# A two-block kernel: the second block's last input projections tied to the delta rule's scan by shared PSUM buffers, and the scan's right-hand side made by one VectorE operation

## The chip, the cores and the metric

The kernel runs on one core of a Trainium2 chip. The metric is the device time of one execution in microseconds, as the median of several runs; the kernel before is at 2178.66 us (three runs, 2176.99 to 2195.75).

## What is computed

Two transformer-like blocks run one after the other on 512 tokens of width 1024. Only the second block's mixer matters here. It projects the normalised tokens into the inputs of three branches (Hyena, gated linear attention or GLA, gated delta rule or GDN), runs the branches and concatenates their outputs. The delta rule works in chunks of 64 tokens, forward and backward at once, with four heads of 96 channels:

```python
rhs = concatenate([kb * exp(gcum), vc * bc])
sol = triangular_solve(eye - a, rhs, lower=True, unit_diagonal=True)
w, u = sol[..., :dk], sol[..., dk:]
v_new = u - w @ s
o = (qc * exp(gcum)) @ s + attn @ v_new
s_new = exp(g_last) * s + einsum('bhjd,bhje->bhde', kc * exp(g_last - gcum), v_new)
```

The state `s` goes from chunk to chunk, so the eight chunks of the 512 tokens follow one another. The kernel applies the inverse to `v - exp(gcum) * (k @ s)`, which is the right-hand side that the change is about.

## The kernel before, in words

The kernel is written as Python generators that emit instructions. `weave` (L331) takes steps from several generators in proportion to given weights, and so sets the order in which work is emitted. The framework then sets each engine's order within the limits of data and buffers: an instruction may be taken ahead of others that were emitted before it if its operands and its buffer are free. On the chip each engine, and the SyncE queue that issues the DMAs, runs its list strictly in order.

The second block's mixer is `mixer_in` (L2097). `side_proj` (L1899) makes 28 input projections of 128 output columns: nine for the delta rule, seven for GLA, then twelve more (`dg0` to `gg2`, six gates, and `hy0` to `hy5`, the Hyena inputs). One projection is `proj2`, which calls `gemm_cm` (L297): the weights of a block come by DMA into `wraw`, ScalarE rounds them (`wh`, L287), VectorE or GpSimd takes the rest (`wl`, L288), and 24 matmuls of 512 columns (lines 293 to 295, eight of each) sum into one PSUM tile `gps`. ScalarE and VectorE then make an activation or a short convolution (`cpad`, L1270; L1277, L1279) of it and a DMA writes it to DRAM.

PSUM tiles are taken by tag; each tag has two buffers, which rotate in the order of emission. `view` renames tags: the mixer's projections run on the view `w`, where "p" and "s" mean "g" and "i" means "p", while the delta rule runs on `v`, where each tag is itself. So before the change the projections sit in the tag "g" and the delta rule uses "p", "s" and "i": the two share nothing.

The first 16 projections and the preparation of keys, values and queries come first, then `gla_general` (behind branches that are not taken here), then `chain()`. It runs `gdn_solve` (L1416) for head pair 0 and then pair 1, and after that `gdn_scan` (L1455). A solve makes its matrices (`dps_`, `kkp`, `qkp`, all tag "p"), and `inverse` (L637) sends them through DRAM, runs 15 short steps of two VectorE operations each (L661, L662), sends the result back through DRAM and finishes with matmuls `ips` (L682). The scan does per chunk and head: `gxp` (keys times state, L1467), `gX` (two VectorE operations, L1470 and L1471), `gup` (inverse times `gX`, L1477), `vd_` and `vn_`, `gsp` (L1491), the new state `gSn` (L1494), and the output `gop` (L1502, L1504; tag "p"), which ScalarE and VectorE combine into `Og` and a DMA writes to `ogd` (L1507). `chain()` is woven with the remaining projections by the weights 192 and 66, after one projection that `next(side)` emits alone.

Behind the scan three generators are woven: GLA (`ttp`, `totp`, `sfp`, `cnp`, ...), `head_norm_out` of the delta rule's output (it loads `hO` from `ogd`, matmuls `ops` at L1949 and L1950), and the Hyena (tables `hraw`, L1818; inputs `hv` from `hud`, L1848; transposes `hyt`; transforms `dfp`; inverse transforms `hip`).

## Time and profile before

| what | us |
|---|---|
| median of three runs | 2178.66 |
| the profiled execution, its own time | 2177.16 |
| its span in the profile | 2175.4 |
| TensorE busy in the span | 1954.9 |
| VectorE busy in the span | 1136.3 |
| last result of the second inverse (`TQ`) starts, from the span's start | 1505.6 |
| last matmul of the scan starts, from the span's start | 1598.5 |
| first load of the stage after the mixer's weave (`g1r`) issues | 1719.0 |

The times on the timeline are from the span's start. The span lies 1.8 us inside the execution's own time, which is 1.5 us under the median. TensorE's busy time tells little by itself, since its clock has two levels, and small matmuls count as busy at either.

### The profile page before, as it was taken

How to read it: one execution, taken by the hardware profiler on the slowest of the kernel's cores; microseconds unless marked ns; L12 is line 12 of the kernel's file. 1: busy time of each engine (PE TensorE's matmuls, PEld its weight loads, DVE VectorE, ACT ScalarE, POOL GpSimd, SP SyncE). 2: the span in 40 equal slices, each digit the busy share in tenths (PEclk: the TensorE clock that was granted, in tenths of full speed). 3: DMA queues.
4: the chain of work that ended last, by engine and by line, in shares of the span. 5: the costliest groups of instructions: out<-in, count | busy, mean ns of one | idle time of the engine just before them, and what ended most of it. 6: DMA issues, size and time to landing. Idle time of an engine off the chain costs nothing. (4 is left out here: it accounts for less than half of the span.)

```text
span 2175.4 us, 37783 instructions
## 1 busy us (share of the span) xinstructions
PE 1954.9 (90%) x15280; PEld 1427.1 (66%) x15280; DVE 1136.3 (52%) x2542; ACT 719.2 (33%) x1390; POOL 245.5 (11%) x254
## 2 busy tenths in 40 slices
PE   7899999999698889988999487899999789999997
PEld 6676767666466764444524266677667577898897
DVE  4565645563362545455461487487456675434433
ACT  4333223333262433121322365422153234312321
POOL 0101011110100211111000031130002150010000
PEclk9999989999799989999999798999579899999999
DMA  6424232432854549979687433332152342333332
GB/s 160 145 61 131 82 102 65 126 111 75 183 175 158 165 133 322 327 262 328 244 300 251 181 116 103 104 81 80 44 171 62 127 144 76 97 93 93 97 92 74
DMA packets 177123, 312.21 MB, mean 144 GB/s; under 512 B 78648, under 2 KB 95816, under 8 KB 176938
## 3 DMA queue, kind: packets, MB, share of 16 engines
q1 hardware_dynamic: 167274, 291.84, 42.6%
q0 software_dynamic: 6784, 10.51, 1.7%
q10 hardware_dynamic: 2880, 7.34, 1.1%
q8 instruction: 123, 2.02, 0.4%
q14 instruction: 62, 0.51, 0.1%
HBM read 278.23 MB, written 39.77 MB: 146 GB/s over the span
## 5 line engine op out<-in xcount | busy, mean ns | idle before, releaser
L288 DVE TENSOR_TENSOR wl<-wraw,wh 128x1024 fp32r<-128x1024 f32 (+2 forms) x215 | 227.9, 1062 | 235.7 <-ACT wh L287 235.3
L287 ACT ACTIVATE wh<-wraw 128x512 fp32r<-128x512 f32 (+2 forms) x233 | 195.7, 844 | 251.7 <-PE gpt L326 136.9
L293 PE MATMUL gps<-hh,wh 128*128 128x512 f32 x568 | 235.2, 415 | 0.4 <-DVE kS L380 0.4
L294 PE MATMUL gps<-hh,wl 128*128 128x512 f32 x568 | 232.5, 410 | 1.2 <-DVE wl L288 1.2
L295 PE MATMUL gps<-hl,wh 128*128 128x512 f32 x568 | 233.0, 411 | 0.0
L1178 PE MATMUL hps<-w,xT 128*64 128x512 f32 x512 | 142.4, 611 | 3.3 <-DMA w<-in_w_moe 3.2
L324 PE MATMUL gpt<-wh,mh 128*128 128x256 f32 x512 | 142.9, 279 | 0.0
L325 PE MATMUL gpt<-wl,mh 128*128 128x256 f32 x512 | 142.9, 279 | 0.0
L326 PE MATMUL gpt<-wh,ml 128*128 128x256 f32 x512 | 142.9, 279 | 0.0
L293 PEld LDWEIGHTS gps<-hh,wh 128*128 128x128 f32 x568 | 108.2, 191 | 29.5 <-issue 2.9
L294 PEld LDWEIGHTS gps<-hh,wl 128*128 128x128 f32 x568 | 107.9, 190 | 29.5 <-DVE wl L288 4.2
L295 PEld LDWEIGHTS gps<-hl,wh 128*128 128x128 f32 x568 | 107.7, 190 | 25.7 <-issue 2.0
L293 PE MATMUL gps<-lhh,wh 128*128 128x512 f32 x232 | 98.0, 424 | 16.7 <-ACT wh L287 6.2
L294 PE MATMUL gps<-lhh,wl 128*128 128x512 f32 x232 | 96.2, 416 | 3.8 <-DVE wl L288 2.2
L324 PEld LDWEIGHTS gpt<-wh,mh 128*128 128x128 f32 x512 | 96.2, 188 | 0.1
L325 PEld LDWEIGHTS gpt<-wl,mh 128*128 128x128 f32 x512 | 96.2, 188 | 0.1
L326 PEld LDWEIGHTS gpt<-wh,ml 128*128 128x128 f32 x512 | 96.2, 188 | 0.0
L295 PE MATMUL gps<-lhl,wh 128*128 128x512 f32 x232 | 95.4, 413 | 0.0
L2003 POOL TENSOR_TENSOR x<-x,xev 128x512 f32<-128x512 f32 x36 | 50.2, 1403 | 388.3 <-DVE xev L2001 388.0
L1178 PEld LDWEIGHTS hps<-w,xT 128*64 128x64 f32 x512 | 36.9, 138 | 66.2 <-issue 50.8
L1279 DVE SCALAR_TENSOR_TENSOR cout<-cpad,cw,cout 128x512 f32<-128x512 f32 (+1 forms) x90 | 66.9, 743 | 2.1
L2019 DVE TENSOR_TENSOR uld<-uld 128x512 f32<-128x512 f32 x32 | 22.2, 693 | 87.3 <-ACT uld L2018 87.3
(1181 smaller groups left out, 4226.9 us busy)
## 6 DMA issues: line engine op xcount, KB each, us to landing
w<-in_w_moe SPq DMA_DIRECT2D x192, 512.0 KB
wraw<-in_w_modb SPq DMA_DIRECT2D x48, 512.0 KB
wraw<-in_w_in_2b SPq DMA_DIRECT2D x41, 512.0 KB
wraw<-in_w_mlp1b SPq DMA_DIRECT2D x32, 512.0 KB
wraw<-in_w_mlp2b SPq DMA_DIRECT2D x32, 512.0 KB
wraw<-in_w_inb SPq DMA_DIRECT2D x31, 512.0 KB
bm<-in_c_bias SPq DMA_DIRECT2D x16, 256.0 KB
wraw<-in_w_inb ACTq DMA_DIRECT2D x8, 512.0 KB
```

The source lines that it names most:

```text
L287: nc.scalar.activation(wh, raw[:, o:o + g], AF.Copy)
L288: self.we.tensor_sub(wl, raw[:, o:o + g], wh)
L293: nc.tensor.matmul(ps, wh, hh, start=first, stop=False)
L294: nc.tensor.matmul(ps, wl, hh, start=False, stop=False)
L295: nc.tensor.matmul(ps, wh, hl, start=False, stop=last)
L324: nc.tensor.matmul(ps, hh[:, g, sl], wh[:, k], start=f, stop=False, skip_group_check=True)
L325: nc.tensor.matmul(ps, hh[:, g, sl], wl[:, k], start=False, stop=False, skip_group_check=True)
L326: nc.tensor.matmul(ps, hl[:, g, sl], wh[:, k], start=False, stop=l, skip_group_check=True)
L1178: nc.tensor.matmul(ps[q], xT[:, 4 * kh + k, q], self.parts[h][:, 512 * (k - 2 * c):512 * (k - 2 * c) + 512], start=kh == 0 and k == 0, sto ...
L1279: nc.vector.scalar_tensor_tensor(ov[:n], pv[:n, :, j:j + L], wcol[:n, j:j + 1], ov[:n], op0=OP.mult, op1=OP.add)
L2003: (nc.gpsimd if last is None or cb < 3 else nc.vector).tensor_add(o, o, t)
L2019: nc.vector.tensor_mul(f, f, f)
```

## The change

Three edits. In `gdn_scan` the negated decays `nG` are made once per call on GpSimd, and the scan's right-hand side is made by one VectorE operation, `gX = xp * nG + v`, where there were two. In `side_proj` the projections from the seventeenth on (those emitted when 16 are there) take the tag "i", which on the view `w` is the tag "p" of the delta rule: their PSUM tiles rotate with `dps_`, `kkp`, `qkp` and `gop`. In `mixer_in` the single `next(side)` ahead of the weave is gone and the weights are 192 to 72.

```diff
--- before.py
+++ after.py
@@ -1459,6 +1459,8 @@
         n = len(heads)
         qs = [slice(64 * d, 64 * d + 64) for d in range(2)]
         St = [self.gS[:, hd[0]] for hd in heads]
+        nG = pool.tile([128, S, 4], F32, name="gnG")
+        nc.gpsimd.tensor_scalar(nG, eG, -1.0, None, op0=OP.mult)
         for c in range(S):
             X, vd, vn = [], [], []
             for i, (h, kT, qT, k, v, E, TQ) in enumerate(heads):
@@ -1467,8 +1469,7 @@
                     nc.tensor.matmul(xp[q], kT[:, c, q], St[i][:, d], start=True, stop=True)
                 x = pool.tile([128, 96], F32, name="gX", bufs=4)
 
-                nc.vector.tensor_scalar(x, xp, eG[:, c, h:h + 1], None, op0=OP.mult)
-                nc.vector.tensor_sub(x, v[:, c], x)
+                nc.vector.scalar_tensor_tensor(x, xp, nG[:, c, h:h + 1], v[:, c], op0=OP.mult, op1=OP.add)
                 X.append(x)
             yield n
             for i, (h, kT, qT, k, v, E, TQ) in enumerate(heads):
@@ -1906,7 +1907,7 @@
             self.we = nc.gpsimd if n in GDN_BLOCKS else nc.vector
             if n == "gk0":
                 pool = later()
-            ps = self.proj2(n, 128, T)
+            ps = self.gemm_cm("w_in_2b", W2.get(n, n), self.hh, self.hl, T, tag="i" if len(self.there) >= 16 else "g")
             if n in GDN_BLOCKS:
                 i = GDN_BLOCKS.index(n)
                 y, d = self.conv_silu(pool, ps, 128, 8, 64, self.cw[:, (i + 6) % 9]), self.cvd[i]
@@ -2149,8 +2150,7 @@
                                 heads.extend((2 * hp + e, kT[:, e], st["q"][:, 2 * hp + e], kv[:, :, e], kv[:, :, 2 + e], E[:, e], TQ[e])
                                              for e in range(2))
                         yield from v.gdn_scan(8, gs, heads, st["g"], self.ogd)
-                    next(side)
-                    self.run(self.weave((chain(), 192), (side, 66)))
+                    self.run(self.weave((chain(), 192), (side, 72)))
                     self.far.close()
                     self.oa = self.ox.enter_context(tp(name="oa", bufs=1, side="right")).tile([128, 8, 384], F32, name="oa")
                     nc.sync.dma_start(self.oa, self.oad.rearrange("c p d -> p c d"))
```

How the order moves. The first place is TensorE ahead of the matmuls `ips` that end the second inverse (pair 1); `gps` are the projections. Before:

```order
L295 MATMUL gps<-lhl,wh 128x512
L293 MATMUL gps<-lhh,wh 128x512
L294 MATMUL gps<-lhh,wl 128x512
L295 MATMUL gps<-lhl,wh 128x512
L682 MATMUL ips<-qv,No 64x64 x32
L682 MATMUL ips<-qv,Z 64x64 x32
L682 MATMUL ips<-W,Z 64x64 x64
L1477 MATMUL gup<-gX,TQ_14195 64x96 x2
L1491 MATMUL gsp<-vd__14284,kv_12336 96x96
```

and of the change, from the end of the first inverse on:

```order
L1478 MATMUL gup<-gX,TQ_13805 64x96 x2
L1478 MATMUL gup<-gX,TQ_13824 64x96 x2
L1503 MATMUL gop<-gS,qT__12141 64x96 x4
L1505 MATMUL gop<-vn__14233,E_13409 64x96 x2
L1505 MATMUL gop<-vn__14240,E_13409 64x96 x2
L1503 MATMUL gop<-gS,qT__12141 64x96 x4
L682 MATMUL ips<-qv,No 64x64 x32
L682 MATMUL ips<-qv,Z 64x64 x32
L682 MATMUL ips<-W,Z 64x64 x64
L1478 MATMUL gup<-gX,TQ_14183 64x96 x2
L1492 MATMUL gsp<-vd__14231,kv_12324 96x96
```

Before, a run of projection matmuls (106 from the last `gop` on, of which four are shown) stands ahead of the second `ips`; now none stands between the `gop` of the first chunk and these `ips`.

The second place is TensorE within one of the later chunks (`gup`, `gsp`, `gop`, `gxp` belong to the scan). Before:

```order
L1477 MATMUL gup<-gX,TQ_13817 64x96 x2
L1477 MATMUL gup<-gX,TQ_13836 64x96 x2
L1491 MATMUL gsp<-vd__14856,kv_12336 96x96 x2
L1477 MATMUL gup<-gX,TQ_14195 64x96 x2
L1504 MATMUL gop<-vn__14858,E_13460 64x96 x2
L1491 MATMUL gsp<-vd__14863,kv_12336 96x96
L1477 MATMUL gup<-gX,TQ_14214 64x96 x2
L1491 MATMUL gsp<-vd__14863,kv_12336 96x96
```

and of the change:

```order
L293 MATMUL gps<-lhh,wh 128x512
L294 MATMUL gps<-lhh,wl 128x512
L295 MATMUL gps<-lhl,wh 128x512
L1478 MATMUL gup<-gX,TQ_13824 64x96 x2
L293 MATMUL gps<-lhh,wh 128x512
L1492 MATMUL gsp<-vd__14976,kv_12324 96x96
L1478 MATMUL gup<-gX,TQ_14183 64x96 x2
L1492 MATMUL gsp<-vd__14976,kv_12324 96x96
L294 MATMUL gps<-lhh,wl 128x512
L1478 MATMUL gup<-gX,TQ_14202 64x96 x2
L1492 MATMUL gsp<-vd__14983,kv_12324 96x96
L295 MATMUL gps<-lhl,wh 128x512
```

Before, the scan's matmuls of chunks 4 to 7 follow one another alone; now 24 projection matmuls lie in each of the chunks 0 to 6, singly among the scan's and in a run at the end of the chunk. In all 288 projection matmuls now stand behind the branches of `gla_general`, where 255 stood.

The third place is SyncE's queue at the end of the scan (`ogd<-Og` is the delta rule's output; `hO` its load; `hv` the Hyena's input). Before:

```order
L1848 DMA hv_15548<-hud 128x512
L1848 DMA hv_15549<-hud 128x512
L2105 DMA lsc<-gv0d 128x512
L1507 DMA ogd<-Og 128x384
L2105 DMA lsc<-gv1d 128x512
L1818 DMA hraw<-in_c_dft 128x512 x2
L2105 DMA lsc<-gv2d 128x512
L1936 DMA hsg_15446<-sgd 128x512
L1936 DMA hsg_15448<-sgd 128x512
L1936 DMA hsg_15450<-sgd 128x512
L1942 DMA hO<-ogd 128x384 x8
L1818 DMA hraw<-in_c_dft 128x512 x2
```

and of the change:

```order
L1508 DMA ogd<-Og 128x384
L2106 DMA lsc<-gv1d 128x512
L1819 DMA hraw<-in_c_dft 128x512
L1586 DMA ls<-lsd 128x1024
L2106 DMA lsc<-gv2d 128x512
L1937 DMA hsg_15404<-sgd 128x512
L1937 DMA hsg_15406<-sgd 128x512
L1937 DMA hsg_15408<-sgd 128x512
L1943 DMA hO<-ogd 128x384 x8
L1819 DMA hraw<-in_c_dft 128x512 x2
L1846 DMA hdk<-in_hy_d 128x2x1 x2
L1849 DMA hv_15506<-hud 128x512
```

Before, the loads of `hv` were issued ahead of the scan's last output, and on TensorE the Hyena's `hyt` and 27 of its `dfp` matmuls stood ahead of the first `ops`. Now `hv` stands behind the eight loads of `hO`, and on TensorE `hyt` and all `dfp` stand behind all 16 `ops`.

## Rows read from the trace of the kernel before

**Rows 1.** the page: the span, and the clock granted to TensorE in 40 slices (tenths)

```profile
span 2175.4 us, 37783 instructions
...
PEclk9999989999799989999999798999579899999999
```

**Rows 2.** windows, scan without projections: PE, weight loads, DVE, ACT, POOL, clock, DMA

```profile
1560.00:1580.00 20.00, 20.00 (x137) 13.22 (x137) 9.55 (x39) 4.13 (x14) 0.00 (x0) 0.50 0.03 11
```

**Rows 3.** windows of 2 us where the clock falls, same columns

```profile
1520.00:1522.00 2.00, 2.00 (x15) 1.40 (x14) 0.80 (x4) 0.23 (x1) 0.00 (x0) 1.00 0.04 8
...
1524.00:1526.00 2.00, 2.00 (x8) 1.19 (x9) 0.36 (x2) 0.00 (x0) 0.00 (x0) 0.50 0.27 98
```

**Rows 4.** the chain that ended last, one chunk to the next, no projections between

```profile
1557.34 1.00 PE gup L1477 x8
...
1568.97 1.00 PE gup L1477 x8
```

**Rows 5.** TensorE timeline: two projection matmuls in a row, then chunks at full clock

```profile
1494.12 0.39 PE L293 MATMUL gps<-lhh,wh 128*128 128x512 f32 x1
1494.35 0.39 PE L294 MATMUL gps<-lhh,wl 128*128 128x512 f32 x1
...
1505.39 0.38 PE L1477 MATMUL gup<-gX,TQ 64*64 64x96 f32 x4
...
1516.64 0.38 PE L1477 MATMUL gup<-gX,TQ 64*64 64x96 f32 x4
...
1517.12 0.50 PE L293 MATMUL gps<-lhh,wh 128*128 128x512 f32 x1
```

**Rows 6.** windows of line 293 alone (every third projection matmul)

```profile
1408.00:1599.40 191.40, 36.10 (x85) 16.38 (x85) 0.79 0.24 68
...
1505.40:1516.60 11.20, 2.01 (x4) 0.74 (x4) 1.00 0.05 18
```

**Rows 7.** VectorE groups during the second inverse (1471.6 to 1487.7): count, busy, mean

```profile
L661 DVE SCALAR_TENSOR_TENSOR tmp<-q,n 128x1 f32<-128x1 f32 (+14 forms) x15 | 4.6, 303 | 2.7 <-DMA n<-nd 2.4
...
L1279 DVE SCALAR_TENSOR_TENSOR sg<-cpad,hcw,sg 128x512 f32<-128x512 f32 x6 | 4.5, 748 | 0.0
...
L662 DVE TENSOR_REDUCE q<-tmp 128x1 f32<-128x1 f32 (+14 forms) x15 | 3.6, 238 | 0.3
...
L288 DVE TENSOR_TENSOR wl<-wraw,wh 128x512 fp32r<-128x512 f32 x5 | 3.4, 687 | 0.0
```

**Rows 8.** VectorE timeline: second inverse starts, its last copy, its last result

```profile
1471.61 0.16 DVE L661 SCALAR_TENSOR_TENSOR tmp<-q,n 128x1 f32<-128x1 f32 x1 [2.40 <-DMA n<-nd]
...
1487.30 0.37 DVE L663 COPY q<-q 128x256 f32<-128x256 f32 x1
...
1505.58 0.69 DVE L702 TENSOR_TENSOR TQ<-ips,qv 128x512 f32<-128x512 f32 x1 [0.24 <-PE ips L682]
```

**Rows 9.** tile view of gX and gsp: ns min/median/max

```profile
L1470 DVE TENSOR_SCALAR gX<-gxp,eG x48: 301/311/320, 908.1 to 1592.9; 128x96 f32<-128x96 f32 x48
...
L1471 DVE TENSOR_TENSOR gX<-kv,gX x48: 241/251/259, 908.4 to 1593.3; 128x96 f32<-128x96 f32 x48
...
L1494 DVE SCALAR_TENSOR_TENSOR gSn<-gSn,eC,gsp x64: 298/309/311, 916.5 to 1588.7; 96x96 f32<-96x96 f32 x64
```

**Rows 10.** timelines of SyncE queue and TensorE behind the scan

```profile
1604.67 6.19 SPq L1942 DMA_DIRECT2D hO<-ogd  x8
...
1599.57 1.08 PE L1858 MATMUL hyt<-ct,hv 128*128 128x128 f32 x4 [0.61 <-DMA hv<-hud]
...
1604.98 0.56 PE L293 MATMUL dfp<-yth,dh 128*128 128x256 f32 x1
...
1611.05 0.86 PE L1949 MATMUL ops<-hO,ct 128*64 128x384 f32 x2 [0.28 <-DMA hO<-ogd]
```

**Rows 11.** windows: the stage behind, once its transforms run

```profile
1622.40:1719.20 96.80, 91.01 (x843) 70.21 (x843) 70.51 (x176) 30.89 (x63) 19.73 (x18) 0.98 0.21 64
```

**Rows 12.** windows: TensorE starting after a pause

```profile
1410.00:1414.00 4.00, 3.65 (x15) 1.86 (x17) 1.04 (x3) 0.89 (x2) 0.00 (x0) 0.53 0.03 8
```

## The prediction

> **What bounds the kernel now.** I read the page first, for where the clock is low. The change touches the second block's mixer, 1410 to 1600 us of a span of 2175.4 us, and the slice of the page that begins at 1523 us has the lowest digit of its PEclk line [rows 1]. The windows say why it matters: with no projections left, TensorE works without a gap at a granted clock of 0.50, the lower of its two levels (1.2 GHz) [rows 2]. It falls after 1522 us [rows 3], about 5 us after the last projections that lie between the chunks' small matmuls (1517.12) [rows 5].
>
> The chain that ended last then shows the scan. One chunk follows the other at a period of 1568.97 - 1557.34 = 11.63 us at the low level [rows 4]. At the full level (2.4 GHz) and with 12 projection matmuls inside, one took 1516.64 - 1505.39 = 11.25 us [rows 5]. Two such matmuls in a row are 0.23 us apart there [rows 5], so the 12 cost 2.8 and the rest of the chunk about 8.5. The scan thus has a small price per chunk at the full clock and pays nearly 12 because little else is left to keep the clock. Line 293 is every third projection matmul: 85 ran between 1408 and 1599.4, 255 projections in all, but only four (12) in that first chunk [rows 6].
>
> Ahead of the scan stands the second inverse. Its 15 steps lie on VectorE, from 1471.61 to 1487.30, and its last `TQ` starts at 1505.58 and ends 0.7 us later [rows 8]. The VectorE groups of that stretch show the steps' own two operations with 4.6 and 3.6 us, and the projections' convolutions and weight splits between them with 4.5 and 3.4 [rows 7].
>
> So three stretches decide: until the second `TQ`, from there to the scan's end at 1599.0 (last matmul at 1598.5 and its half microsecond), and the stage behind, which ends at 1719.0.
>
> **Part 1, until the second `TQ`.** Projections leave the second inverse. VectorE's steps alone are 4.6 + 3.6 = 8.2 us of 15.7 [rows 7, 8], so up to 7.5 us go. Against that, 24 instead of 12 projections stand ahead of one of the first solve's small matmuls: 12 x 0.23 = +2.8 us. TensorE is also idle for some 20 us of the second inverse, and starts its `ips` at the low level: after an earlier pause a window of 4 us had a clock of 0.53 [rows 12]. The `ips` are 8 us of matmuls at the full level, of which the first part would double; I take +2 (0 to +8). The 33 projections that are now behind the branches instead of ahead (33 x 0.23 = 7.6 us) I value at -1: the low clock just behind the branches [rows 12] says that TensorE had paused ahead of them, so it was not what they waited for; -7.6 is the other end. Sum: -7.5 + 2.8 + 2 - 1 = -3.7. The chain from the inverse through DRAM has fewer other transfers beside it, for which I allow 2 more: **-6** (-12 to 0).
>
> **Part 2, the scan.** After the change 24 projections lie in each of the first seven chunks. At the full clock a period is 8.5 + 24 x 0.23 (5.5) = 14.0 us. The merged right-hand side takes one operation out of each of 48 pairs. The two cost 311 and 251 ns [rows 9]; one operation of the same form, a scalar_tensor_tensor that reads PSUM, costs 309 at 96 x 96 [rows 9]. So 0.25 us goes from VectorE each time; 32 of the 48 are in this scan, four to a chunk, and on a chain that ends on TensorE perhaps one in each chunk counts: -0.2. The bounds are 0 and all four, -1.0. The new `nG` is one small GpSimd operation a call, three in all, ahead of the scans, where GpSimd has nothing that the scan waits for: nothing. Period 13.8; seven make 96.6, and the last chunk without projections about 4: now, by the period, it begins at 1568.97 + 2 x 11.63 = 1592.2 and takes 6.8 us at the low level, of which little more than half is left at the full one: 100.6 us against 1599.0 - 1506.3 = 92.7 now: **+8**. Here 168 projections stand where 24 stood, so 144 x 0.23 = 33 us of work enter the stretch, and 25 of them come back by the clock. The buffers: `gop` and the next projection rotate over two PSUM tiles, so a `gop` waits until the projection before last is read out. The read is one ScalarE or VectorE operation of 0.7 us while a block takes TensorE 5.5; hidden. If it were not, TensorE in order would stand still at the `gop`, 0.7 in each of seven chunks, +5.
>
> **Part 3, the stage behind.** `hv` is now issued behind the eight `hO`, whose issue takes from 1604.67 to 1610.86 [rows 10], 12 us after the scan's end. From the first `hO` issue to the first `ops` it took 6.4 us [rows 10], so `hyt` starts about 18 us after the scan's end instead of 0.6 (1599.57), and the transforms `dfp`, 5.4 us behind it, 23 instead of 6.0 [rows 10]. TensorE gets the transposes and `ops` meanwhile, work that it did behind the transforms before. Later TensorE is 91.01 of 96.8 us busy [rows 11], so what it does earlier is saved there, and what it stands idle is lost. It has some 12 us of such work for the 17 us of delay, and some of its old idle time is there: **+4** (0 to +8).
>
> **Elsewhere** 16 of the merged operations lie in earlier scans, from 908 us on [rows 9]: 16 x 0.25 = 4 us of VectorE. I take 0 (-4 to +2), since nothing says that VectorE ends a wait there.
>
> **Sum.** -6 + 8 + 4 = +6 on the profiled execution's 2177.16, hence 2183 us; that execution is 1.5 us below the median of 2178.66. Own range 2175 to 2191.
>
> **Rivals.** First, on the slower side: the clock doesn't stay up. In the trace it fell 5 us after the projections had become rare [rows 3, 5]; in the changed order each chunk has a run of projections at its end and a part of about 8 us in which they are single. If the clock falls in each such part, 3.7 us of the run are at the low level (+1.85) and the chain's small matmuls lose about 1.1: 3 in each chunk, 7 x 3 = +21, so 2204. It decides if the projections singled between the scan's matmuls are too few to keep the level. For it speaks that 12 in the first chunk held it [rows 5] but only until shortly after; against it, that now there are twice as many, in every chunk. Its far end is a low clock throughout: 11.6 + 24 x 0.46 = 22.6 us a chunk, 8.8 more than 13.8, times seven +62: 2245. The Trainium skill, "TensorE: Matmul & The Clock Gate", section "HAM oscillation — how this bites in real kernels", tells of such a loop: bursts of matmuls with gaps between them start every burst at the low level, so that the transition is paid in each iteration instead of once. By that rule this rival would be the case; its gaps are waits for DMA, and here small matmuls fill them. The trace so far shows a level held with 12 and lost with none, which leaves it open.
>
> Second, on the faster side: the projections fill waits. If of the 12 further ones in a chunk two thirds fall where TensorE waits for VectorE between `gup` and `gsp`, the period is 11.25 + 4 x 0.23 = 12.1: seven and 4 are 88.7, that is -4; with the full -6 of part 1 and -2 for a Hyena delay that the pulled-ahead work fills, 2165. For it: VectorE and ScalarE stand between any two matmuls of a head. Against it: four heads' matmuls already interleave.
>
> Third, the change does little of what it says: projections in the second inverse were filling idle time on TensorE and the 7.5 us of part 1 return as waits for DMA, while the period stays near 13; then 0 + 0 + 0: 2177.
>
> **How the numbers follow.** Forecast 0.45, clock rival 0.17, filling rival 0.20, nothing 0.18. A measurement of this kernel can tell about 1%, that is below 2156.9 or above 2200.4 us. The forecast and the third case lie within it altogether; the filling rival at 2165 passes the lower bound only if all its terms err one way (a quarter, 0.05); the clock rival at 2204 lies beyond the upper one in three of four (0.13). That leaves 0.82 for no difference. The range reaches from a little under the filling rival to a little over the clock rival's price, 2163 to 2206, and leaves the low clock throughout, and a gain in all three parts, outside.
>
> **What would show it.** In the changed kernel's profile: the second `TQ` about 6 us earlier, near 1500; a chunk period near 13.8 at a clock near 1.00 in the windows of the scan; the scan's end at about 1601; the first `dfp` 23 us after the scan's end; `g1r` near 1725. Wrong would be: a window of a chunk with a clock near 0.5 (first rival), a period of 12 (second), a `TQ` that is not earlier (third, or the inverse waits for its DMA), `gop` with an idle time ended by a projection's read-out (the shared buffers).

## The result, and the profile after

The changed kernel takes 2214.48 us (median of four executions, 2201.52 to 2225.84) against 2181.26 for the kernel before beside it: a ratio of 1.0136, 95% interval 1.0088 to 1.0183. The forecast was 2183 with a range of 2163 to 2206. The change is slower by 1.4%, some 30 us, about five times the 6 us that were expected, and its median is outside the range. Each ratio below is to executions of the kernel before that ran beside that experiment; their medians lay between 2179.20 and 2186.97. Medians are of all executions, and the ratios leave out those more than 1.5% above the shortest of the same kernel: three of filler_w100, and the profiled one of filler_gx, which ran at a lower clock throughout and whose trace is not read.

The page of the profiled execution of the changed kernel (2217.19 us), its span and the clock granted to TensorE in 40 slices:

```profile
span 2215.4 us, 37718 instructions
...
PEclk9999999999799979999999799887979999999999
```

The span is 40.0 us longer than in [rows 1], and the lowest digit of the mixer's slices is 7, no longer the 5 of before: the scan runs at a higher clock on average and still takes longer.

A first thing to settle is where to measure from. At the first `gup` of the program (in the earlier, four-chunk scans, ahead of which next to nothing is changed) the two profiles stood at 909.6 and 913.1 us already, and the experiments between 906 and 921. A second profile of the kernel before (before_again, below) had its first `gup` at 923.2 and from there on repeated every stretch within 1 us or so: 1264.7 us to the end of the span against 1265.8. So the first 900 us vary by more than 10 us from one execution to the next, and times are compared from the first `gup` on. Even so, the stretch from there to the branches, 498.8 and 498.6 us in the two profiles of the kernel before, lay between 494.0 and 502.9 in the experiments, which hardly differ there; whether the program or the execution makes that is open. A difference of a few us "to the end" is therefore not much to go by, and the stretches behind the branches are the better measure. All stretches below are read in this way from the timelines (starts of `gup`, `gt`, `TQ`, the last issue of `ogd`, and `g1r`):

| from, to | before | again | changed |
|---|---|---|---|
| first `gup` to the end of the span | 1265.8 | 1264.7 | 1302.3 |
| behind the branches (first `gt`) to the second `TQ` | 97.1 | 96.1 | 95.2 |
| second `TQ` to the last `ogd` (the scan) | 94.2 | 94.1 | 113.8 |
| last `ogd` to `g1r` (the stage behind) | 119.2 | 119.4 | 137.7 |
| `g1r` to the end | 456.4 | 456.5 | 456.4 |

The loss in these profiles is 36.5 us: +19.6 in the scan and +18.5 in the stage behind, -1.9 in the solves, and +0.4 between the first `gup` and the branches.

**The second inverse** got shorter, as expected. VectorE's timeline of the changed kernel (start, duration, what; its first step, its last copy, the last result):

```profile
1480.35 0.16 DVE L661 SCALAR_TENSOR_TENSOR tmp<-q,n 128x1 f32<-128x1 f32 x1 [2.89 <-DMA n<-nd]
...
1489.47 0.38 DVE L663 COPY q<-q 128x256 f32<-128x256 f32 x1
...
1507.52 0.69 DVE L702 TENSOR_TENSOR TQ<-ips,qv 128x512 f32<-128x512 f32 x1 [0.24 <-PE ips L682]
```

The steps take 1489.47 - 1480.35 = 9.1 us instead of 15.7 [rows 8]. The last result stands 95.2 us behind the branches all the same, since the first inverse got longer: its `TQ` starts 57.2 us behind them (1469.49) where it had been 51.8. From the last copy to the first `ips` it took 7.8 us (1489.47 to 1497.28) instead of 9.4 (1487.30 to 1496.72). TensorE had stood idle for 19 us by then, and the `ips` begin at the low level, as foreseen, and are at the full one from 1504 on (windows below, with the granted clock third from the end of each line). They take 10.2 us in one piece, where the chain of before has two pieces with a VectorE step between, 8.8 us from the first start to the last end.

The chain that ended last in the changed kernel (start, us, what) with three windows of it, and the chain in the kernel before:

```profile
1497.28 10.22 PE ips L682 x256
```

```profile
1500.00:1502.00 2.00, 2.00 (x43) 2.00 (x41) 0.00 (x0) 0.60 (x1) 0.00 (x0) 0.50 0.00 0
1502.00:1504.00 2.00, 2.00 (x63) 1.94 (x62) 1.13 (x2) 0.00 (x0) 0.00 (x0) 0.90 0.01 4
1504.00:1508.00 4.00, 4.00 (x124) 3.76 (x118) 2.81 (x5) 0.00 (x0) 0.00 (x0) 1.00 0.02 4
```

```profile
1496.72 4.02 PE ips L682 x128
1500.77 0.69 DVE W L693
1501.51 4.02 PE ips L682 x128
```

**The scan.** Windows of the changed kernel (PE, weight loads, DVE, ACT, POOL with their counts, granted clock, DMA share, GB/s), cut where the clock changes:

```profile
1508.00:1512.50 4.50, 4.28 (x32) 2.68 (x31) 3.00 (x12) 1.36 (x4) 0.00 (x0) 1.00 0.01 4
1512.50:1519.00 6.50, 6.50 (x17) 4.67 (x17) 0.78 (x3) 0.60 (x1) 0.00 (x0) 0.51 0.08 30
1519.00:1540.00 21.00, 19.03 (x158) 13.35 (x156) 11.39 (x35) 6.44 (x18) 0.15 (x2) 0.99 0.19 58
1540.00:1553.00 13.00, 13.00 (x53) 8.77 (x52) 3.98 (x14) 1.37 (x4) 0.00 (x0) 0.50 0.20 61
1553.00:1621.00 68.00, 65.09 (x487) 40.55 (x485) 37.17 (x113) 20.59 (x53) 0.59 (x8) 0.98 0.22 74
```

TensorE is idle for only 5.1 of these 113 us, and at 1.00 for much of them. But twice it is at the low level: for 6.5 us from 1512.5 on, and for 13 us ahead of and in the third run of projections. When the first fall came, no projection had run since 1472 and until 1511.3; the level came back at 1519, within the first chunk's run of projections. The TensorE timeline of the same kernel shows the second fall (start, duration; lines 293 to 295 are projections):

```profile
1521.31 0.40 PE L295 MATMUL gps<-lhl,wh 128*128 128x512 f32 x1
...
1529.75 0.50 PE L293 MATMUL gps<-lhh,wh 128*128 128x512 f32 x1
...
1535.10 0.39 PE L295 MATMUL gps<-lhl,wh 128*128 128x512 f32 x1
...
1538.00 0.41 PE L1492 MATMUL gsp<-vd__14526,kv 64*96 64x96 f32 x4 [0.32 <-DVE vd__14526 L1480]
...
1539.97 0.63 PE L1492 MATMUL gsp<-vd__14533,kv 64*96 64x96 f32 x2
...
1548.46 0.79 PE L293 MATMUL gps<-lhh,wh 128*128 128x512 f32 x1
...
1553.32 0.52 PE L295 MATMUL gps<-lhl,wh 128*128 128x512 f32 x1
1553.68 0.40 PE L293 MATMUL gps<-lhh,wh 128*128 128x512 f32 x1
...
1572.08 0.50 PE L293 MATMUL gps<-lhh,wh 128*128 128x512 f32 x1 [0.16 <-DVE Og L1507]
...
1572.75 0.38 PE L1478 MATMUL gup<-gX,TQ 64*64 64x96 f32 x4
1573.06 0.50 PE L295 MATMUL gps<-lhl,wh 128*128 128x512 f32 x1
```

The first run of projections ends at 1521.31. Then the small matmuls of a chunk stand alone until the next run, of 24, at 1529.75: 8.1 us plus a run of 5.7, the 13.8 of the forecast. The next gap begins at 1535.10, and at 1539.97 a `gsp` that had taken 0.41 takes 0.63: the level has fallen. It comes back only within the next run, between 1553.32 (0.52) and 1553.68 (0.40), after 13 us at half speed. From 1557 on it looks different: projections stand in ones, twos and threes among the scan's matmuls, with a run at the chunk's end, and the level holds (0.98). The order that was shown with the change is of such a later chunk. In the second and third chunks the 24 stand in one run with nothing but small matmuls between the runs.

**The stage behind.** SyncE's queue, and TensorE, in the changed kernel:

```profile
1626.42 5.75 SPq L1943 DMA_DIRECT2D hO<-ogd  x8
...
1634.84 0.87 SPq L1849 DMA_DIRECT2D hv<-hud  x2
```

```profile
1625.11 1.94 PE L1298 MATMUL ttp<-ct,cfb 128*128 128x128 f32 x8 [4.63 <-DVE cfb L1287]
...
1638.10 1.56 PE L1950 MATMUL ops<-hO,ct 128*64 128x384 f32 x4
...
1648.37 0.38 PE L1859 MATMUL hyt<-ct,hv 128*128 128x128 f32 x2
...
1653.50 0.58 PE L293 MATMUL dfp<-yth,dh 128*128 128x256 f32 x1 [1.90 <-ACT hyf L1861]
```

`hO` is issued from 1626.42 on, `hv` at 1634.84, 13.5 us after the last `ogd` (1621.31). But `hyt` starts 27 us behind that `ogd` and `dfp` 32 us, where 18 and 23 were forecast. From the issue of `hv` to `hyt` it is 13.5 us, and TensorE did not wait ahead of `hyt`: it had the transposes, `ops` and `sfp` to do from 1636.20 on, without a gap. Two windows each of the changed kernel and of the kernel before, from the scan's end on:

```profile
1622.00:1660.00 38.00, 27.53 (x128) 20.93 (x129) 12.40 (x35) 18.61 (x40) 0.00 (x0) 0.64 0.62 209
1660.00:1760.00 100.00, 92.83 (x836) 71.22 (x836) 67.43 (x161) 28.37 (x57) 19.03 (x18) 0.95 0.15 47
```

```profile
1600.00:1638.00 38.00, 35.20 (x237) 28.95 (x235) 21.07 (x51) 26.19 (x52) 3.09 (x2) 0.89 0.70 228
1638.00:1719.00 81.00, 76.33 (x721) 56.19 (x721) 57.54 (x145) 18.98 (x43) 16.64 (x17) 0.98 0.13 40
```

In the first 38 us TensorE idles 10.5 us instead of 2.8, and what it does, it does at a mean clock of 0.64 instead of 0.89. Counting busy time times the missing clock as lost, that is 9.9 against 3.9. In the rest it idles 7.2 against 4.7 and loses 4.6 against 1.5. The differences, 7.7 + 6.0 + 2.5 + 3.1 = 19.3, account for the 18.5 of the stage.

### The profile page after: what moved, and what is told of

Its sections match the earlier page's. It is cut to its first block, busy times and chain, and to the rows that moved or that the text cites. A ratio compares the mean times of both kernels' runs of the same rounds, so it can differ in the third digit from the quotient of the medians.

```text
span 2215.4 us, 37718 instructions
## 1 busy us (share of the span) xinstructions
PE 1947.4 (88%) x15280; PEld 1420.9 (64%) x15280; DVE 1126.1 (51%) x2494; ACT 723.2 (33%) x1392; POOL 245.8 (11%) x257
## 5 line engine op out<-in xcount | busy, mean ns | idle before, releaser
L293 PE MATMUL gps<-lhh,wh 128*128 128x512 f32 x232 | 99.5, 431 | 10.6 <-ACT wh L287 4.6
```

The lines of the kernel that those rows point to most:

```text
L293: nc.tensor.matmul(ps, wh, hh, start=first, stop=False)
```

## The experiments

In the table, the last three columns are from the profiled execution; "to the end" begins at the first `gup`, "scan" and "behind" are the stretches of the table above.

| run | median us | ratio to before (95%) | to the end | scan | behind |
|---|---|---|---|---|---|
| kernel before | 2181.26 | | 1265.8 | 94.2 | 119.2 |
| changed kernel | 2214.48 | 1.0136 (1.0088 to 1.0183) | 1302.3 | 113.8 | 137.7 |
| gx_only | 2197.38 | 1.0066 (1.0032 to 1.0100) | 1276.4 | 103.0 | 115.5 |
| tie_only | 2217.41 | 1.0138 (1.0083 to 1.0193) | 1294.7 | 117.7 | 129.0 |
| weight100 | 2207.72 | 1.0111 (1.0069 to 1.0154) | 1283.2 | 114.9 | 113.3 |
| weight200 | 2208.64 | 1.0097 (1.0065 to 1.0129) | 1294.7 | 110.4 | 106.6 |
| hO_own_queue | 2215.81 | 1.0105 (1.0060 to 1.0150) | 1296.3 | 116.7 | 131.7 |
| after_filler | 2222.89 | 1.0149 (1.0102 to 1.0196) | 1304.4 | 123.8 | 130.7 |
| change_filler | 2208.57 | 1.0101 (1.0035 to 1.0167) | 1299.1 | 113.4 | 131.0 |
| change_w100_filler | 2190.02 | 1.0014 (0.9984 to 1.0044) | 1277.9 | 104.7 | 118.2 |
| filler_gup | 2209.05 | 1.0112 (1.0066 to 1.0157) | 1289.2 | 126.7 | 116.6 |
| filler_gup_gsp | 2179.33 | 0.9983 (0.9954 to 1.0012) | 1257.1 | 83.8 | 126.5 |
| filler_w84 | 2192.87 | 1.0028 (0.9996 to 1.0060) | 1277.0 | 112.5 | 112.0 |
| filler_w100 | 2190.95 | 0.9979 (0.9932 to 1.0026) | 1249.6 | 86.3 | 116.2 |
| filler12_w100 | 2176.09 | 0.9962 (0.9932 to 0.9992) | 1258.7 | 95.4 | 111.3 |
| filler_gx | 2238.39 | 1.0212 (1.0157 to 1.0268) | | | |

**before_again**: the kernel before, unchanged, for a second profile.

> The kernel before once more, for a second profile. Theory N (the 3.5 to 10 us by which the changed kernels are late ahead of any changed instruction, at the first gup, come from execution to execution): its first gup lies anywhere from 909 to 920 us. Rival: within 1 us of 909.6, so that the lateness belongs to the changed programs. The scan (94.2 us from the last TQ to the last ogd) and the stage behind (119.2) repeat within 2 us by both.

Measured: first `gup` at 923.2, 3 us beyond the range of theory N and further from 909.6 than any changed program but for filler_gx; scan 94.1, stage behind 119.4. So a lateness of that size ahead of the first `gup` needs no change of the program.

### The parts of the change

**gx_only**: the kernel before with `nG` and the one-operation `gX` alone (the lines of `gdn_scan` in the diff).

> The kernel before with the merged right-hand side alone. Theory A (the merged operation is worth little; the loss is in where the projections lie): within 5 us of before. Rival: the merged operation itself takes or gives more than 10 us, by a wait on nG or on the PSUM read.

Measured: 0.66% slower, and 10.6 us more from the first `gup` on, some 8 of them behind the branches: +8.8 in the scan, +3.1 from the branches to the second `TQ`, -3.7 in the stage behind. Neither theory holds: the operation was not harmless, and no wait on `nG` or on the read of PSUM appears in the trace; VectorE's merged operations take 0.31 us, as they were priced. What changed is the order on TensorE. The scan holds 24 projections as before, the last 41.3 us behind the second `TQ` instead of 38.3. They lie otherwise: of the periods between the issues of `ogd` the second fell from 21.0 to 18.1 us, and the third, which now has five projections at the low clock where it had none, grew from 11.2 to 16.5. From the second `TQ` to the end of the third period that makes +3 us. The other 6 are in the chunks behind, which hold no projections (and, in gx_only, eight `hyt` of the Hyena, 3.3 us). Two `gup` groups, one chunk apart, in gx_only's TensorE timeline:

```profile
1585.98 1.31 PE L1478 MATMUL gup<-gX,TQ 64*64 64x96 f32 x8
...
1598.71 0.91 PE L1478 MATMUL gup<-gX,TQ 64*64 64x96 f32 x8
```

That is 12.7 us, with no wait on TensorE between them, where the same matmuls took 11.63 [rows 4]. They stand in another order, and fewer of them overlap. That the order does it is argued from these rows, not shown by a run.

**tie_only**: shared buffers and weights of the change, with the right-hand side in two operations.

```diff
-            ps = self.proj2(n, 128, T)
+            ps = self.gemm_cm("w_in_2b", W2.get(n, n), self.hh, self.hl, T, tag="i" if len(self.there) >= 16 else "g")
...
-                    next(side)
-                    self.run(self.weave((chain(), 192), (side, 66)))
+                    self.run(self.weave((chain(), 192), (side, 72)))
```

> The changed kernel with the two-operation right-hand side: shared buffers and weights alone. Theory T (the tie carries the loss; the merged operation alone only shifts the order of small matmuls): the scan takes 108 to 116 us, the stage behind 130 to 138, total 2205 to 2216, like the change. Rival G (the merged operation carries about half, as its run alone with +17 suggests, and the parts add): total 2195 to 2201.

Measured: 2217.41, as slow as the whole change. Of the two theories T holds, each figure within 2 us of its range (scan 117.7, stage behind 129.0). Together with the tie the merged operation costs nothing more; alone it does. The parts don't add; both change the order on TensorE. (tie_only has the shared buffers, the weights and the dropped `next(side)` together; these three were not run one by one.)

### Late projections and the stage behind

**weight100**: the change with `(side, 100)` in place of `(side, 72)`.

> The changed kernel with weights 192 to 100: buffers shared as in the change, but the projections end about two chunks before the scan does (58 stand ahead of the second ips, 120 in the scan). Theory A (the stage behind is late because the projections end with the scan): the scan's end to the stage's end back from 137.7 to about 120 us, total about 2195. Rival B (the shared buffers themselves, wherever the projections lie): 2205 or more, stage behind unchanged.

Measured: 2207.72. The stage behind came back to 113.3, even below before, and the issue of `hv` to 1592.3, far ahead of the scan's last `ogd`. So the late end of the projections is what the stage behind paid for. But the scan stayed at 114.9 where it should have shrunk: with the projections gone the clock fell there too, as two windows of weight100 show, and some of the Hyena's work had moved into it (first `dfp` 3.6 us ahead of the last `ogd`). Scan and stage behind together are 23 us shorter than in the change. Each theory got one half right.

```profile
1590.00:1610.00 20.00, 19.90 (x137) 13.10 (x136) 8.96 (x30) 5.96 (x17) 0.00 (x0) 0.51 0.31 99
1610.00:1630.00 20.00, 18.71 (x108) 12.42 (x105) 10.19 (x35) 7.38 (x22) 0.00 (x0) 0.50 0.18 51
```

**hO_own_queue**: in the change, `nc.sync.dma_start(O[:, c], od[c])` becomes `nc.gpsimd.dma_start(O[:, c], od[c])`.

> The changed kernel with the eight loads of hO issued by GpSimd instead of SyncE. Theory A1 (hv and the tables are late because they stand behind hO in SyncE's queue): first dfp 6 to 8 us earlier after the scan, total 4 to 8 us less. Rival (the DMA engines are full there, or the Hyena's inputs come late whatever the queue): first dfp within 2 us of where it was, total the same.

Measured: first `dfp` 27.8 us behind the last `ogd` instead of 32.2, the stage 6.0 shorter, and no difference in the median (2215.81) beyond the interval of its ratio. Both theories' numbers missed: SyncE's queue is a part of the delay, the smaller one; the DMA engines' share of 0.62 over those 38 us (window of the changed kernel above) and the transposes at the low clock are still there.

**weight200**: the change with `(side, 200)`; all 288 projections stand ahead of the second `ips`.

> The changed kernel with weights 192 to 200: buffers shared, but all 288 projections stand ahead of the second ips. Theory A (position, not sharing, costs): scan 90 to 98 us at the low clock, stage behind 113 to 120, the time from the first gup to the end within 8 us of the kernel before's 1265. Rival B (sharing costs wherever the projections lie): the solves longer by 20 us or more, total over 2200.

Measured: 2208.64. Scan and stage behind are 217.0 together, against 213.4 before and 251.5 in the change: there theory A nearly holds (its single figures miss, since the Hyena's transforms moved into the scan), but to the end it is 29 us longer than before, where theory A had at most 8. The second `TQ` came 118.8 us behind the branches instead of 97.1, 21.7 more, which is what rival B had said, and the total is over its 2200. 57 projections more (288 for 231) are 57 x 0.23 = 13 of it; whether the shared buffers make the rest was not separated.

### The clock

**after_filler**: the change with two idle 128x128 matmuls ahead of each `gop`. These, and the idle matmuls below, write into unused columns of a PSUM tile; their product is not read.

```diff
-                    op = self.ps.tile([128, 2, 96], F32, name="gop", tag="p", bufs=2)
+                    ow = self.ps.tile([128, 512], F32, name="gop", tag="p", bufs=2)
+                    op = ow[:, :192].rearrange("p (a d) -> p a d", a=2)
+                    for z in range(2):
+                        nc.tensor.matmul(ow[:, 256:384], self.C["ident"], self.C["ident"], start=True, stop=True)
```

> The changed kernel with 64 idle 128x128 matmuls more in the scan (two ahead of each gop, into unused columns of its PSUM tile; their product is not read). Theory A (the first chunks are long because the clock falls between the runs of projections): first three chunk periods from 18.8, 18.7 and 23.4 us to 14 to 16, total 10 to 15 us less. Rival B (shared buffers make gop and projections wait): periods the same or longer, total the same or up to 10 us more.

Measured: periods 20.1, 19.6, 23.9 and then 16.4 in place of 14.7, scan 123.8. The theory's numbers failed; but so did its means. The clock still fell in the same places:

```profile
1540.00:1550.00 10.00, 9.33 (x63) 6.35 (x62) 4.51 (x17) 1.82 (x6) 0.15 (x2) 0.66 0.26 80
1550.00:1560.00 10.00, 10.00 (x51) 7.15 (x47) 2.97 (x8) 2.43 (x5) 0.00 (x0) 0.83 0.05 20
```

Ahead of the `gop` the idle matmuls lie at the two ends of a gap between runs: in the gap in which the clock fell, at 1543, none stands between 1539.4 and 1545.2.

**filler_gup** and **filler_gup_gsp**: the kernel before, no edit of the change, with one idle matmul ahead of each head's `gup`, and in the second also of each head's `gsp`.

```diff
-                up = self.ps.tile([128, 96], F32, name="gup", tag="s", bufs=2)
+                uw = self.ps.tile([128, 512], F32, name="gup", tag="s", bufs=2)
+                up = uw[:, :96]
+                if od is not None:
+                    nc.tensor.matmul(uw[:, 256:384], self.C["ident"], self.C["ident"], start=True, stop=True)
...
-                    sp = [self.ps.tile([96, 96], F32, name="gsp", tag="i", bufs=2) for _ in range(2)]
+                    sw = [self.ps.tile([128, 512], F32, name="gsp", tag="i", bufs=2) for _ in range(2)]
+                    sp = [t[:96, :96] for t in sw]
+                    if od is not None:
+                        nc.tensor.matmul(sw[0][:, 256:384], self.C["ident"], self.C["ident"], start=True, stop=True)
```

> The kernel before with one idle 128x128 matmul ahead of each head's gup (four to a chunk; the product is not read), no edit of the change. Theory A (a chunk costs some 8 us at the full clock and 11.6 at the low one, and full-width matmuls spread over the chunk hold the clock): granted clock 1.00 through the scan, periods near 9.5, total 8 to 14 us less than before. Rival (four are too few, or the clock falls all the same): clock 0.50, periods 12.5, total 5 to 10 us more.

> The same with one more ahead of each head's gsp (eight to a chunk). Theory A: granted clock 1.00, periods near 10.5, total 2 to 8 us less than before. Rival: clock 0.50, periods 13.5 to 14, total 12 to 20 us more.

Measured: with four the clock fell, and the idle matmuls came on top at half speed: scan 126.7, 1.1% slower. That is the rival's case, at periods of 16.6 to 19.7 instead of its 12.5. Not all of the 32.5 us are the idle matmuls: from their starts to the next instruction they take 18, and ten more projections (34 for 24) and some of the Hyena's work lie in the scan too. With eight, and again 34 projections, it held through the whole scan, which went from 94.2 to 83.8 us; the periods are 10.5 to 14.1. Windows of the three kernels (before_again, four, eight), within the scan:

```profile
1535.00:1612.00 77.00, 74.03 (x474) 47.71 (x474) 37.25 (x142) 16.75 (x52) 0.00 (x0) 0.50 0.16 54
```

```profile
1525.00:1630.00 105.00, 105.00 (x531) 65.12 (x528) 39.93 (x147) 17.52 (x53) 0.15 (x2) 0.50 0.16 53
```

```profile
1510.00:1590.00 80.00, 79.71 (x696) 53.31 (x696) 46.65 (x173) 19.93 (x58) 0.15 (x2) 1.00 0.13 44
```

More work and less time: 80 us at 1.00 hold 696 matmuls, 105 us at 0.50 hold 531. The gain of 10.4 us was mostly given back in the stage behind (126.5, first `dfp` 27.2 us after the last `ogd`): here too the projections had spread into later chunks and the loads of `hv` stood behind `hO`. The median is that of before, not 2 to 8 us less.

**change_filler**: the change with the same eight idle matmuls a chunk.

> The changed kernel with one idle 128x128 matmul ahead of each head's gup and gsp (eight to a chunk), the places at which they held the clock in the kernel before. They add about 8 x 0.21 = 1.7 us to a chunk. Theory A (the change's first chunks are long because the clock falls between the runs of projections): granted clock 1.00 from 1520 us on, periods 15 to 16.5 in all chunks instead of 18.8, 18.7, 23.4 and then 13.3 to 14.7; scan within 3 us of the change's 113.8. Rival B (shared buffers make the first chunks long): first three periods 20 to 25 at clock 1.00, scan about 125.

Measured: clock 1.00 from the second `TQ` to the scan's end,

```profile
1505.00:1520.00 15.00, 15.00 (x110) 10.96 (x108) 7.87 (x24) 3.79 (x9) 0.00 (x0) 1.00 0.14 41
1520.00:1540.00 20.00, 19.91 (x166) 14.36 (x162) 10.35 (x33) 5.80 (x16) 0.15 (x2) 1.00 0.12 43
1540.00:1553.00 13.00, 13.00 (x85) 9.58 (x81) 6.48 (x19) 3.25 (x8) 0.15 (x2) 1.00 0.38 115
1553.00:1618.00 65.00, 63.28 (x503) 43.57 (x501) 32.74 (x101) 18.10 (x48) 0.44 (x6) 1.00 0.20 69
```

scan 113.4 as against 113.8, while eight idle matmuls a chunk were added, for which 1.7 us were expected. The periods between the issues of `ogd` are 16.4, 14.8, 22.7, 16.0, 16.0, 15.8: the first three together 53.9 instead of 60.9, the next three 47.8 instead of 42.7. The third missed the expected 15 to 16.5: the issue of an `ogd` follows the `gop`, which slip against the chunks, so that this period holds 50 projections (48 in the change). The later chunks, at the full level in both kernels, got 5.1 / 3 = 1.7 us longer each. By that price the fillers cost 7 x 1.7 = 12 us in the scan, and the low clock cost the change's scan about as much. (From its start to the next instruction an idle matmul takes 0.35 us in those chunks; the difference of the periods is less than eight of these, so part of it fills time between other matmuls.) Rival B's 125 us did not come.

**change_w100_filler**: eight idle matmuls and `(side, 100)`.

> The changed kernel with weights 192 to 100 and eight idle matmuls a chunk: projections end earlier, and the clock is held. Theory A (the change's loss is the low clock in the scan plus the late Hyena; both are removed here at the price of 8 x 0.21 = 1.7 us a chunk): scan at clock 1.00, 100 to 106 us (weight100: 114.9), stage behind 113 to 118, first gup to end 1265 to 1275, against 1302 for the change. Rival (what weight100 and the change lose in the scan isn't the clock): scan 115 or more at clock 1.00.

Measured: 2190.02, a ratio of 1.0014, against 1.0136 for the change; scan 104.7 at a clock of 1.00, stage behind 118.2, 1277.9 to the end (3 us above what was expected). With the two causes taken away, and the shared buffers still there, the loss is gone from the median. In the profile 12 us of it are left, 10.5 of them in the scan, which holds 120 projections and the idle matmuls.

```profile
1510.00:1610.00 100.00, 99.67 (x804) 70.80 (x804) 55.50 (x173) 33.11 (x86) 0.59 (x8) 1.00 0.27 87
```

**filler_w84**, **filler_w100** and **filler12_w100**: the kernel before with eight idle matmuls and `(side, 84)` or `(side, 100)` in place of `(side, 66)`; the last also with one ahead of each `gop`.

> The kernel before with eight idle matmuls a chunk, and weights 192 to 84, so that the projections end earlier and the Hyena's loads of hv stand ahead of the scan's last outputs again. Theory A (the filler's gain in the scan, 10 us, was given back because the Hyena's loads fell behind the scan): scan 84 to 88 us, stage behind 115 to 120, total 8 to 12 us less than before. Rival (the stage behind grows because the scan ends earlier and its loads take their time): stage behind 126 again, total the same as before.

> The same with weights 192 to 100. By theory A like the run with 84, within 4 us; by the rival total as before.

> The kernel before with twelve idle matmuls a chunk (one more ahead of each gop) and weights 192 to 100. With eight, executions lay between 2161 and 2205 us: in the slow ones the clock fell within the scan. Theory A: twelve hold it in all executions, for 4 x 0.21 = 0.8 us a chunk more: all executions within 15 us of each other, median 2165 to 2180. Rival: the spread stays over 30 us.

Measured: filler_w100's profiled execution is the shortest of all from the first `gup` on, 1249.6 us, with the scan at 86.3 and the stage behind at 116.2, as theory A said. There the clock held in the last chunks too, in which no projections are left:

```profile
1545.00:1596.00 51.00, 49.69 (x470) 35.10 (x471) 33.73 (x128) 22.39 (x60) 0.00 (x0) 1.00 0.39 125
```

But its ten executions lie between 2161.34 and 2204.55, and their median, 2190.95, is no shorter than that of the kernel before beside it (2186.97). filler_w84 missed theory A, with a scan of 112.5 and no gain in the median. Its profiled execution shows why: the clock held until 1562 and not behind it.

```profile
1509.00:1562.00 53.00, 53.00 (x446) 35.95 (x440) 30.04 (x108) 12.47 (x36) 0.15 (x2) 1.00 0.08 26
1562.00:1620.00 58.00, 58.00 (x314) 38.44 (x311) 23.50 (x82) 14.04 (x40) 0.00 (x0) 0.51 0.27 86
```

The mean granted clock that is on record for each execution points the same way for filler_w100: 0.943 to 0.949 in its three shortest executions, 0.925 to 0.929 in its three longest.

With twelve the executions lie within 21 us (2168.69 to 2189.40; 15 were expected) and the median is 2176.09, ratio 0.9962 with an interval that ends just below 1: a version faster than both kernels, by 0.4%, with no edit of the change in it. The kernel before beside it spread over 25 us.

**filler_gx**: filler_gup_gsp with the merged operation.

> The kernel before with eight idle matmuls a chunk and the merged right-hand side. Theory O (alone, the merged operation lost about 9 us in the scan because it changes the order of small matmuls while they run at the low clock): with the clock held, the scan within 3 us of the 83.8 of the same filler without it, and first gup to end within 4 us of 1257. Rival M (the merged operation itself delays gup): scan 4 to 9 us longer than 83.8.

Measured: 2238.39, 2.1% slower, far outside both theories. The record of the clock points to why: its mean is 0.917 to 0.921 in the other four executions, where filler_gup_gsp has 0.943 to 0.950 and filler_gup, whose clock fell, 0.922 to 0.927. So the level was probably not held, which both theories had as their condition. Without a trace to read, that, and why the merged operation costs what it does alone, stay open.

## Why the prediction was wrong

**Part 1 was right in its mechanism, with one term too small.** VectorE's steps lost 6.6 of the 7.5 us. The `ips` paid 2.2 of the low level (2 were taken), of which 1.4 count, since the wait for the VectorE step between them went away. The way through DRAM ahead of them, for which I had allowed 2 us, got 1.6 shorter. The first inverse got 5.4 longer instead of 2.8; what the other 2.6 are stays open. The 33 projections ahead of the branches, valued at -1, gave nothing that shows: the stretch up to the branches is 0.4 longer. In all -1.9 instead of -6, inside the bounds of -12 to 0.

**Part 2 failed in the sentence "At the full clock a period is 8.5 + 24 x 0.23".** Where the clock was full the period was right: 13.8 at 1521 to 1535, 13.3 to 14.7 in the later chunks. But the sum took the full clock for every chunk. It fell in the first chunk, as its first projections came, and again in the gap behind the run at 1529.75. The windows show it: 6.5 us at 0.51 and 13 us at 0.50 are 3.2 + 6.5 = 9.7 us lost; 11.6 are missing between +8 and +19.6, and change_filler prices it at some 12. With the level held and the fillers taken off at that price, change_filler's scan is about the 100.6 that I had. So the work in the scan was sized rightly and the level was not. I had also read the order of a later chunk, with single projections between the scan's matmuls, as that of all; the level fell where there were none, or only the first.

That is the first rival, which I had with 0.17 and 3 us a chunk: it came in two places, not in all seven chunks, and cost 3.2 and 6.5. In the second the chain's small matmuls alone were at 0.50 from 1540 to 1548.46, 4.2 us lost where I had 1.1, and the run that followed stayed there for 5.0 us, 2.5 lost where I had 1.85. The forecast of 2204 for that rival was nearer to the 2214 than my own, but it had the loss in other places and left part 3 as it was.

The Trainium skill, "TensorE: Matmul & The Clock Gate", section "HAM oscillation — how this bites in real kernels", says that bursts of matmuls with waits for DMA between them begin at the low level each time. The trace agrees for the run at 1548.46 (0.79, then 0.63 a matmul), and does not for the run at 1529.75, which began at the full level (0.50, then 0.39) behind a gap of 8 us; in both gaps TensorE was busy with small matmuls.

**Part 3 failed in "It has some 12 us of such work for the 17 us of delay".** I let that work count in full as saved later, and put the start of `hyt` at 18 us, 12 to the issue of `hv` and 6.4 from there. They were 13.5 and 13.5, so 27: the waiting work stood ahead of `hyt` in TensorE's order, and was itself a chain of transposes with waits for VectorE and DMA between, at a mean clock of 0.64. TensorE's waits in that stretch (line, what it waited for, us in total, times, longest) were

```profile
PE ttp L1298 <- DVE cfb L1287: 6.3, 2, 4.6
PE totp L1595 <- DMA ls<-lsd: 2.1, 1, 2.1
PE dfp L293 <- ACT hyf L1861: 1.9, 1, 1.9
PE hyt L1859 <- ACT hyf L1861: 1.7, 1, 1.7
```

Idle time and low clock are 10.2 and 9.1 us of the difference; I had 4 for both. weight100 and change_w100_filler, with the Hyena early again, show that it was the lateness: 113.3 and 118.2.

**The merged operation** was costed at -0.2 a chunk with bounds of 0 and -1.0. Alone it cost +10.6 us: the bounds held only what VectorE does, and left out that the framework orders TensorE anew around it. That the order is what cost is argued, not shown. In the change it did not show.

**The rivals.** The faster one (projections fill waits, 2165) had its sign wrong: TensorE is idle for 5.1 of the scan's 113 us, so there was little to fill, and a projection moved there is added time. The third was wrong in that the tie matters greatly. The shared buffers as such, a term of +5 at most, made waits of 1.2 us in all in the change's scan (`gop` and `gps` for the read-out of `Og`). The sign that I had named came once ahead of it, a `gop` that waited for the read-out of a projection:

```profile
1475.28 0.58 PE L1503 MATMUL gop<-gS,qT__12141 96*64 96x96 f32 x4 [2.51 <-DVE sg L1926]
```

Behind it TensorE stood idle for 19 us, so this wait cost nothing. What they cost in weight200's solves is open.

## What to carry to other kernels

When work moves beside a chain of small matmuls, write down for each stretch at which of TensorE's two levels it would run, with the time at each; a sum at one level is a bound, not a forecast. Where other work is to hold the clock, look at where it lies in the loop and not only at its sum: here it fell between runs of 24 projections at the chunks' ends, and eight small idle matmuls spread over the chunk held it in four of the five profiles that can be read, though not in every execution. And work that ends later delays the loads of the next stage, and puts other work ahead of them in TensorE's order; price the whole stage behind at its own clock.

## What was not expected of the hardware

In filler_gup TensorE was busy 105 of 105 us, with four idle matmuls a chunk, and stayed at 0.50; in filler_gup_gsp, with eight, at 1.00 for 80 us. I had expected four to do. In the other direction, the level of the changed kernel rose from 0.50 to 1.00 while TensorE did nothing but the `ips`, matmuls of 64 x 64. And the same program spread widely: filler_w100's executions lie 43 us apart, and with twelve idle matmuls 21. The longer ones had the lower mean clock (0.928 at 2204.55 us, 0.949 at 2161.34); that it is the scan in which it fell is likely from the trace of filler_w84, but no trace of such an execution shows it.
